# Four transposes for a tile's queries and keys, and a swapped copy written across partitions

## The chip, the cores and the metric

The kernel runs on one core of one Trainium2 chip. The metric is the device time of one execution, in microseconds (us), lower is better. The core has TensorE (PE, with its weight loads PEld), VectorE (DVE), ScalarE (ACT), GpSimd (POOL) and SyncE (SP), whose queue starts the transfers. Each takes its own instructions in order; they wait for each other by semaphores.

## The reference

A decoder of two layers on 1024 tokens of 1024 features: gated linear attention and an MLP, then differential attention and an MLP. The change is inside differential attention, eight heads, each with two components of 64 features:

```python
q = rms_norm((xn @ w_q).reshape(B, S, DIFF_HEADS, 2, DIFF_DH), q_gain) * (DIFF_DH ** -0.5)
...
s = jnp.einsum('bhcqd,bhckd->bhcqk', q_blk, k).astype(jnp.float32)
...
p = jax.nn.softmax(s, axis=-1)
a = p[:, :, 0] - lam * p[:, :, 1]
return jnp.einsum('bhqk,bhkv->bhqv', a.astype(v.dtype), v)
```

Keys are normed in the same way, and the mask is causal in blocks of 128 tokens. Float32 inputs go through the matmul as sums of a high part (rounded) and a low part (the rest).

## The kernel before

Attention runs over 64 tiles: head h, then 128 tokens t = 0 to 7. A tile is the generator `attn_tile`, cut by its `yield`s into pieces. Pieces 0 to 7 are its projection (L112 to L114: 8 groups of three matmuls); one unit of the program is the projection of one tile. The later pieces of earlier tiles are hung between the groups by the table STEPS: piece 11 of tile j stands two units later behind the second group, its scores (piece 12) a unit and a position behind that, the weighting (13), the transposes of the weights (14, L898), the product with v (15, L903) and the last scaling (16, L910) after that. PE's order is that of the program; ACT, DVE and POOL are ordered at build time by a scheduler.

The pieces that matter, in the order of their lines:

- L833 to L838: squares of q and k (ACT), sums (DVE, L836), the norm (POOL, L837, L838). L842 (DVE) multiplies, L844 (POOL) applies the gain.
- L847 to L849 write the tile `split`: for each of four blocks of 64 features (two of q, two of k) the high part, the low part, and for q once more the high part. So columns 0 to 127 of a block are [high, low], and columns 64 to 191 are [low, high].
- L854 and L857: six transposes. The two of k go to one bank of PSUM (`pk`), the four of q to another (`pq`). The pool `ms` has two banks, so a tile takes both.
- L859 (ACT) copies k to `kt`, L861 (DVE) the four columns of q to `qs`.
- L871 and L872: for each component, [high, low] of q times keys [high, low], and then [low, high] of q times the same keys. Together that is the full product.
- L881 (DVE) takes the minimum, L883 (ACT) the exponential and its sum, L888 to L891 (DVE) weigh one component against the other, L893, L907 and L908 (POOL) are the norm of the output, which L910 (ACT) applies.

At each of the seven head changes three of the next head's four weight tiles are split, and the first tile of the head after that (the first of the next head was done a head earlier): L97 loads `raw` (two buffers), L100 (POOL) multiplies it by the gains, L104 (ACT) writes the high part, L105 (DVE) the low part. The buffers of `raw` and of the weights come free only as the old head's weights are used up, so these twelve instructions and the loads fall into some 15 us. At the seventh change there is no head after the next, so there are no gains to multiply for it.

Of the kernel before, what the change touches and what calls it, by code (L numbers as in the profile page):

```python
# [6 lines left out]
F32 = mybir.dt.float32  # L7
F32R = mybir.dt.float32r
# [5 lines left out]
P = 128  # L14
# [8 lines left out]
AH, DH, VD = 8, 64, 128  # L23
# [17 lines left out]
def trunk(tc, io, out):  # L41
    nc = tc.nc
    with ExitStack() as es:
# [11 lines left out]
        def big():  # L55
            return pp.tile([P, 1024], F32, tag="big", name="big", bufs=2)
# [4 lines left out]
        def mst():  # L61
            return pp.tile([P, 512], F32, tag="ms", name="ms", bufs=2)

        def slot(name, dt=F32, shape=(P, 1024)):
            return sp.tile(list(shape), dt, tag="S", name=name, bufs=13)

        def half(name, dt=F32, shape=(P, 512)):
            return mp.tile(list(shape), dt, tag="M", name=name, bufs=16)
# [8 lines left out]
        identr = cp.tile([P, P], F32R, name="identr")  # L77
# [61 lines left out]
        def tcols(t):  # L139
            return slice(t * P, (t + 1) * P)  # L140
# [578 lines left out]
        for h in range(GH):  # L719
# [11 lines left out]
            d = 2 if h == 0 else 0  # L731
# [88 lines left out]
        def attn_tile(i):  # L820

            h, t = divmod(i, T)
            if t == 0:
                KV[h] = attn_kv()
            kt, vt = KV[h]
# [17 lines left out]
                                 s4.unsqueeze(2).broadcast_to([P, 4, DH]))  # L843
            nc.gpsimd.tensor_mul(qk[:, 0:P], qk[:, 0:P], gq)  # L844
            yield
            sp_ = slot("split", F32R)[:, 0:768].rearrange("p (a d) -> p a d", d=3 * DH)
            nc.scalar.copy(sp_[:, :, 0:DH], qk4)  # L847
            nc.vector.tensor_sub(sp_[:, :, DH:2 * DH], qk4, sp_[:, :, 0:DH].bitcast(F32))
            nc.scalar.copy(sp_[:, 0:2, 2 * DH:3 * DH], sp_[:, 0:2, 0:DH].bitcast(F32))  # L849
            yield  # L850
            pq = mst()
            pk = mst()
            for c in range(2):
                nc.tensor.transpose(pk[:, tcols(c)].bitcast(F32R), sp_[:, 2 + c, 0:P], identr)  # L854
            for c in range(2):
                for v in range(2):
                    nc.tensor.transpose(pq[:, tcols(2 * c + v)].bitcast(F32R), sp_[:, c, v * DH:v * DH + P], identr)  # L857
            for c in range(2):
                nc.scalar.copy(kt[c][:, tcols(t)], pk[:, tcols(c)])  # L859
            qs = half("qs", F32R)  # L860
            nc.vector.tensor_copy(qs, pq)  # L861
            yield
            nb = 1 if L <= 512 else 2
            B = L // nb
# [1 line left out]
            for c in range(2):  # L866
                sc = big().rearrange("p (n i) -> p n i", n=2)[:, 0:nb, 0:B]
                for n in range(nb):
                    keys = kt[c][:, n * B:(n + 1) * B]
                    lastb = n == nb - 1  # L870
                    nc.tensor.matmul(sc[:, n, :], lhsT=qs[:, tcols(2 * c)], rhs=keys, start=True, stop=False)  # L871
                    nc.tensor.matmul(sc[:, n, :], lhsT=qs[:, tcols(2 * c + 1)], rhs=keys, start=False, stop=not lastb)  # L872
                    if lastb:
                        nc.tensor.matmul(sc[:, n, B - P:B], lhsT=identb, rhs=causal, start=False, stop=True)
                scs.append(sc)
# [3 lines left out]
            for c in range(2):  # L879
                sc = scs[c]  # L880
# [9 lines left out]
            a = pr[0]  # L890
# [30 lines left out]
        def piece(j, n):  # L921
            if n == 0:
                live[j], done[j] = attn_tile(j), 0
            assert done[j] == n, (j, done[j], n)
            next(live[j])
            done[j] += 1
# [101 lines left out]
```

## Time and profile before

| | us |
|---|---|
| median of three runs | 2353.85 |
| lowest, highest | 2353.66, 2354.66 |
| the profiled execution | 2351.53 |
| its span, first to last instruction | 2349.7 |
| attention stage | about 1130 to 1640 |

The profiled execution is 2.3 us under the median. The stage is read best in periods of one head, 62.8 us each (ACT's cast L104 behind a head change starts at 1296.10, 1358.90 and 1421.70). The views used are the page, the windows, the waits and the timeline of each engine at one head change, the third (1290 to 1312 us).

### The profile page before, as it was taken

The page shows a single profiled execution, that of the slowest core. Times are in us where ns is not written, and L with a number is a line of the kernel's source. Part 1 is how long each engine was busy: PE and PEld are TensorE (multiplying, and loading weights), DVE is VectorE, ACT ScalarE, POOL GpSimd, SP SyncE. Part 2 cuts the span into 40 slices and gives each one's busy share as a digit, 9 for nine tenths or more (in the row PEclk, how much of TensorE's full clock was granted, in tenths as well). Part 3 has the DMA queues.
Part 4 walks back from the last instruction along what each step waited for, and adds up shares of the span by engine and source line. Part 5 has one row for each costly group of instructions (what it writes and reads, how often), then busy time and mean ns, then how long its engine had stood idle before and what let it go on. Part 6 is the DMA issues. An engine that isn't in the chain of part 4 may idle for free.

```text
span 2349.7 us, 31435 instructions
## 1 busy us (share of the span) xinstructions
PE 2309.7 (98%) x11710; PEld 1965.5 (84%) x11710; DVE 1490.4 (63%) x2336; ACT 1108.9 (47%) x2162; POOL 580.6 (25%) x807
## 2 busy tenths in 40 slices
PE   9999999999999999999999999999999999999999
PEld 6888888878888888887999999998878888888887
DVE  7766566478838556474666666666478838556474
ACT  6434333257335354353555555565257335354352
POOL 0253242000401103004455555543000401103002
PEclk9999999999999999999999999999999999999999
DMA  4111114667173361632101111113767173371631
GB/s 156 48 36 52 39 52 169 216 234 290 57 255 118 120 236 57 221 102 76 59 25 36 37 36 36 36 42 130 248 236 284 57 255 118 120 238 54 215 112 68
DMA packets 97831, 292.42 MB, mean 124 GB/s; under 512 B 11696, under 2 KB 24752, under 8 KB 97680
## 3 DMA queue, kind: packets, MB, share of 16 engines
q1 hardware_dynamic: 97680, 290.43, 36.1%
q8 instruction: 92, 1.51, 0.3%
q14 instruction: 59, 0.48, 0.1%
HBM read 227.47 MB, written 62.91 MB: 124 GB/s over the span
## 4 chain that ended last, share of the span: by engine, by line
PE 90%; POOL 3%; ACT 3%; DVE 2%; issue 1%; DMA 1%; SPq 0%; POOLq 0%; ACTq 0%
PE big L518 9%; PE big L522 8%; PE big L520 8%; PE mm L112 7%; PE mm L113 7%; PE mm L114 7%; PE ms L518 4%; PE ms L520 4%; PE ms L522 4%; PE mm L522 4%; PE mm L518 4%; PE mm L520 4%; PE ms L903 2%; PE big L352 2%; POOL raw L100 2%; PE big L871 1%
## 5 line engine op out<-in xcount | busy, mean ns | idle before, releaser
L518 PE MATMUL big<-oph 128*128 128x512 f32 x896 | 348.9, 389 | 0.0
L522 PE MATMUL big<-oph,opl 128*128 128x512 f32 x896 | 348.6, 389 | 0.0
L520 PE MATMUL big<-opl,oph 128*128 128x512 f32 x896 | 348.6, 389 | 0.0
L537 DVE TENSOR_TENSOR opl<-wq,oph 128x1024 fp32r<-128x1024 f32 x144 | 172.6, 1230 | 157.8 <-ACT oph L536 149.1
L537 POOL TENSOR_TENSOR opl<-hsum,oph 128x1024 fp32r<-128x1024 f32 x16 | 42.1, 2653 | 873.1 <-ACT oph L536 873.1
L536 ACT CAST oph<-wq 128x1024 fp32r<-128x1024 f32 x144 | 145.3, 1051 | 206.3 <-issue 76.8
L518 PEld LDWEIGHTS big<-oph 128*128 128x128 f32 x896 | 168.2, 188 | 35.2 <-DVE h L436 0.4
L520 PEld LDWEIGHTS big<-opl,oph 128*128 128x128 f32 x896 | 168.2, 188 | 34.9
L522 PEld LDWEIGHTS big<-oph,opl 128*128 128x128 f32 x896 | 168.2, 188 | 34.9
L112 PE MATMUL mm<-whi,x2h 128*128 128x384 f32 x512 | 188.9, 369 | 0.0
L518 PE MATMUL ms<-oph 128*128 128x512 f32 x448 | 175.2, 391 | 0.0
L520 PE MATMUL ms<-opl,oph 128*128 128x512 f32 x448 | 174.8, 390 | 0.0
L518 PE MATMUL mm<-oph 128*128 128x512 f32 x448 | 174.7, 390 | 0.0
L522 PE MATMUL ms<-oph,opl 128*128 128x512 f32 x448 | 174.6, 390 | 0.0
L522 PE MATMUL mm<-oph,opl 128*128 128x512 f32 x448 | 174.3, 389 | 0.0
L520 PE MATMUL mm<-opl,oph 128*128 128x512 f32 x448 | 174.3, 389 | 0.0
L114 PE MATMUL mm<-whi,x2l 128*128 128x384 f32 x512 | 172.4, 337 | 0.0
L113 PE MATMUL mm<-wlo,x2h 128*128 128x384 f32 x512 | 171.8, 335 | 0.0
L537 POOL TENSOR_TENSOR opl<-hc,oph 128x512 fp32r<-128x512 f32 x96 | 124.3, 1329 | 131.7 <-ACT oph L536 131.7
L536 ACT CAST oph<-ws 128x1024 fp32r<-128x1024 f32 x80 | 80.6, 1052 | 159.5 <-PE big L520 80.5
L537 DVE TENSOR_TENSOR opl<-ws,oph 128x1024 fp32r<-128x1024 f32 x80 | 94.9, 1218 | 75.8 <-ACT oph L536 75.8
L536 ACT CAST oph<-hc 128x512 fp32r<-128x512 f32 x160 | 88.2, 620 | 86.2 <-PE ms L520 58.3
(253 smaller groups left out, 5476.5 us busy)
## 6 DMA issues: line engine op xcount, KB each, us to landing
wq<-in_mlp_w SPq DMA_DIRECT2D x128, 512.0 KB, 4.6
oph<-xd SPq DMA_DIRECT2D x84, 512.0 KB, 5.9
opl<-xd SPq DMA_DIRECT2D x84, 512.0 KB, 7.2
h<-h SPq DMA_DIRECT2D x48, 512.0 KB, 4.3
xd<-oph SPq DMA_DIRECT2D x28, 512.0 KB, 3.6
xd<-opl SPq DMA_DIRECT2D x28, 512.0 KB, 4.6
raw<-in_w_qkv SPq DMA_DIRECT2D x32, 384.0 KB, 3.0
raw<-in_w_vg SPq DMA_DIRECT2D x16, 512.0 KB, 3.6
```

What stands on the lines that cost most here:

```text
L100: nc.gpsimd.tensor_mul(v, v, g)
L112: nc.tensor.matmul(ps, lhsT=l[0][ls], rhs=r[0][rs], start=first, stop=False)
L113: nc.tensor.matmul(ps, lhsT=l[0][ls], rhs=r[1][rs], start=False, stop=False)
L114: nc.tensor.matmul(ps, lhsT=l[1][ls], rhs=r[0][rs], start=False, stop=last)
L352: nc.tensor.matmul(blocks(sc, l), lhsT=w, rhs=second(w, s), start=True, stop=True)
L518: nc.tensor.matmul(banks[m], lhsT=lh[ls], rhs=rh[rs], start=one, stop=False, skip_group_check=not start)
L520: nc.tensor.matmul(banks[m], lhsT=lh[ls], rhs=rl[rs], start=False, stop=False, skip_group_check=not start)
L522: nc.tensor.matmul(banks[m], lhsT=ll[ls], rhs=rh[rs], start=False, stop=end, skip_group_check=not start)
L536: nc.scalar.copy(h_, s)
L537: eng.tensor_sub(l_, s, h_.bitcast(F32))
L871: nc.tensor.matmul(sc[:, n, :], lhsT=qs[:, tcols(2 * c)], rhs=keys, start=True, stop=False)
L903: nc.tensor.matmul(po[:, 0:P], lhsT=aT[:, tcols(j)], rhs=vt[:, j, :], start=(j == 0), stop=(j == t))
```

## The change

A tile's `split` keeps only [high, low] for each of the four blocks and moves to the pool `half`. Four transposes, keys first, write one bank (`pqk`). ACT copies the two of k. DVE copies the two of q as they are, and then partitions 64 to 127 of q to partitions 0 to 63 of the other half of `qs`; ACT copies partitions 0 to 63 to 64 to 127. That gives [low, high] without a transpose. In the built program the reads of the bank by two engines stand in a row: DVE's first copy waits for ACT's second copy of k, and ACT's copy of q waits for DVE's second.

```diff
--- before.py
+++ after.py
@@ -843,22 +843,20 @@
                                  s4.unsqueeze(2).broadcast_to([P, 4, DH]))
             nc.gpsimd.tensor_mul(qk[:, 0:P], qk[:, 0:P], gq)
             yield
-            sp_ = slot("split", F32R)[:, 0:768].rearrange("p (a d) -> p a d", d=3 * DH)
+            sp_ = half("split", F32R).rearrange("p (a d) -> p a d", d=2 * DH)
             nc.scalar.copy(sp_[:, :, 0:DH], qk4)
             nc.vector.tensor_sub(sp_[:, :, DH:2 * DH], qk4, sp_[:, :, 0:DH].bitcast(F32))
-            nc.scalar.copy(sp_[:, 0:2, 2 * DH:3 * DH], sp_[:, 0:2, 0:DH].bitcast(F32))
             yield
-            pq = mst()
-            pk = mst()
+
+            pqk = mst()
+            for a in (2, 3, 0, 1):
+                nc.tensor.transpose(pqk[:, tcols(a)].bitcast(F32R), sp_[:, a, :], identr)
             for c in range(2):
-                nc.tensor.transpose(pk[:, tcols(c)].bitcast(F32R), sp_[:, 2 + c, 0:P], identr)
-            for c in range(2):
-                for v in range(2):
-                    nc.tensor.transpose(pq[:, tcols(2 * c + v)].bitcast(F32R), sp_[:, c, v * DH:v * DH + P], identr)
-            for c in range(2):
-                nc.scalar.copy(kt[c][:, tcols(t)], pk[:, tcols(c)])
+                nc.scalar.copy(kt[c][:, tcols(t)], pqk[:, tcols(2 + c)])
             qs = half("qs", F32R)
-            nc.vector.tensor_copy(qs, pq)
+            nc.vector.tensor_copy(qs[:, 0:256], pqk[:, 0:256])
+            nc.vector.tensor_copy(qs[0:DH, 256:512], pqk[DH:P, 0:256])
+            nc.scalar.copy(qs[DH:P, 256:512], pqk[0:DH, 0:256])
             yield
             nb = 1 if L <= 512 else 2
             B = L // nb
@@ -868,8 +866,8 @@
                 for n in range(nb):
                     keys = kt[c][:, n * B:(n + 1) * B]
                     lastb = n == nb - 1
-                    nc.tensor.matmul(sc[:, n, :], lhsT=qs[:, tcols(2 * c)], rhs=keys, start=True, stop=False)
-                    nc.tensor.matmul(sc[:, n, :], lhsT=qs[:, tcols(2 * c + 1)], rhs=keys, start=False, stop=not lastb)
+                    nc.tensor.matmul(sc[:, n, :], lhsT=qs[:, tcols(c)], rhs=keys, start=True, stop=False)
+                    nc.tensor.matmul(sc[:, n, :], lhsT=qs[:, tcols(2 + c)], rhs=keys, start=False, stop=not lastb)
                     if lastb:
                         nc.tensor.matmul(sc[:, n, B - P:B], lhsT=identb, rhs=causal, start=False, stop=True)
                 scs.append(sc)

```

Behind the change lines are two lower: L879 is L881 of before, L881 is L883, L886 to L889 are L888 to L891, L891 is L893, L897 is L899, L904 to L908 are L906 to L910. L853 are the four transposes, L855 the copies of k, L857 and L858 DVE's copies of q, L859 is now ACT's copy of q.

PE's order is the same but for the transposes. The scheduler orders the other three engines anew around them. First POOL at the third head change (raw: weights before their gains; so and el: norm of the output; s: norm of q and k), before:

```order
L844 TENSOR_TENSOR qk<-qk,gq 128x128
L893 TENSOR_SCALAR el<-l 128x1
L907 TENSOR_SCALAR so<-so,el 128x1
L908 TENSOR_TENSOR so<-so,nhalf 128x1
L100 TENSOR_TENSOR raw<-raw,g_qkv 128x768
L837 TENSOR_SCALAR s_11330<-s_11330,e_b_473 128x4
L838 TENSOR_TENSOR s_11330<-s_11330,nhalf 128x4
L100 TENSOR_TENSOR raw<-raw,g_qkv 128x768
L844 TENSOR_TENSOR qk<-qk,gq 128x128
L100 TENSOR_TENSOR raw<-raw,g_qkv 128x768
L893 TENSOR_SCALAR el<-l 128x1
L907 TENSOR_SCALAR so<-so,el 128x1
```

And now:

```order
L891 TENSOR_SCALAR el<-l 128x1
L844 TENSOR_TENSOR qk<-qk,gq 128x128
L100 TENSOR_TENSOR raw<-raw,g_qkv 128x768
L905 TENSOR_SCALAR so<-so,el 128x1
L906 TENSOR_TENSOR so<-so,nhalf 128x1
L837 TENSOR_SCALAR s_11285<-s_11285,e_b_473 128x4
L838 TENSOR_TENSOR s_11285<-s_11285,nhalf 128x4
L100 TENSOR_TENSOR raw<-raw,g_qkv 128x768 x2
L891 TENSOR_SCALAR el<-l 128x1
L844 TENSOR_TENSOR qk<-qk,gq 128x128
L905 TENSOR_SCALAR so<-so,el 128x1
L906 TENSOR_TENSOR so<-so,nhalf 128x1
```

L844 went behind el, the first L100 ahead of the two instructions on so, and the second L844 and el behind both later L100.

DVE at the same place (nm: minimum of the scores; rho and p: weighing; wlo: low part of a weight), before:

```order
L861 CAST qs<-ms 128x512
L842 TENSOR_TENSOR qk<-mm,s_11210 128x256
L105 TENSOR_TENSOR wlo<-raw,whi 128x768
L881 TENSOR_REDUCE nm<-big 128x1 x2
L105 TENSOR_TENSOR wlo<-raw,whi 128x768
L888 RECIPROCAL rho<-l 128x1
L889 SCALAR_TENSOR_TENSOR rho<-rho,nlam,l 128x1
L891 SCALAR_TENSOR_TENSOR p<-p,rho 128x640
L848 TENSOR_TENSOR split<-qk,split 128x4x64
L836 TENSOR_REDUCE s_11330<-qsq 128x4
L105 TENSOR_TENSOR wlo<-raw,whi 128x768
L861 CAST qs<-ms 128x512
```

And now:

```order
L105 TENSOR_TENSOR wlo<-raw,whi 128x768
L857 CAST qs<-ms 128x256
L858 CAST qs<-ms 64x256
L879 TENSOR_REDUCE nm<-big 128x1 x2
L842 TENSOR_TENSOR qk<-mm,s_11167 128x256
L105 TENSOR_TENSOR wlo<-raw,whi 128x768
L886 RECIPROCAL rho<-l 128x1
L887 SCALAR_TENSOR_TENSOR rho<-rho,nlam,l 128x1
L889 SCALAR_TENSOR_TENSOR p<-p,rho 128x640
L848 TENSOR_TENSOR split<-qk,split 128x4x64
L105 TENSOR_TENSOR wlo<-raw,whi 128x768
L836 TENSOR_REDUCE s_11285<-qsq 128x4
```

L842 stood ahead of the first L105 and now stands behind it, the two copies of q and the two minima; the sum for s (L836) went from ahead of the third L105 to behind it.

ACT at the same place (whi: high part of a weight), before:

```order
L910 ACTIVATE oo<-ms,so 128x128
L849 CAST split<-split 128x2x64
L833 ACTIVATE qsq<-mm 128x256
L104 CAST whi<-raw 128x768
L834 ACTIVATE vt<-mm,r_b_465 128x128
L899 COPY aT<-big 128x640
L859 CAST kt<-ms 128x128 x2
L104 CAST whi<-raw 128x768
L883 ACTIVATE p,l<-big,nm 128x768 x2
L906 ACTIVATE oo,so<-ms 128x128
```

And now:

```order
L908 ACTIVATE oo<-ms,so 128x128
L104 CAST whi<-raw 128x768
L833 ACTIVATE qsq<-mm 128x256
L834 ACTIVATE vt<-mm,r_b_465 128x128
L897 COPY aT<-big 128x640
L855 CAST kt<-ms 128x128 x2
L104 CAST whi<-raw 128x768
L859 CAST qs<-ms 64x256
L881 ACTIVATE p,l<-big,nm 128x768 x2
L904 ACTIVATE oo,so<-ms 128x128
```

The third cast of a weight went ahead of the squares (qsq), and the new copy of q stands between the fourth cast and the exponentials.

## Rows read from the trace of the kernel before

**Rows 1.** Two lines of the page: the busy time of the engines (part 1), and the chain that ended last, by engine (part 4).

```profile
PE 2309.7 (98%) x11710; PEld 1965.5 (84%) x11710; DVE 1490.4 (63%) x2336; ACT 1108.9 (47%) x2162; POOL 580.6 (25%) x807
...
PE 90%; POOL 3%; ACT 3%; DVE 2%; issue 1%; DMA 1%; SPq 0%; POOLq 0%; ACTq 0%
```

**Rows 2.** The view by windows, for the stretch of the third head change and for the rest of the period behind it. Columns: stretch, its length, busy us of PE, PEld, DVE, ACT and POOL (instructions), granted clock, DMA share, GB/s.

```profile
1296.00:1312.00 16.00, 14.51 (x98) 13.53 (x97) 10.90 (x19) 10.30 (x29) 11.50 (x13) 1.00 0.33 104
1312.00:1358.00 46.00, 46.00 (x313) 43.27 (x312) 27.09 (x58) 26.68 (x89) 20.93 (x40) 1.00 0.04 11
```

**Rows 3.** The view of waits, TensorE alone, over the attention stage (1130 to 1640 us). Columns: who waited and for whom, us in total, times, longest us.

```profile
PE big L871 <- ACT aT L899: 5.3, 7, 0.8
PE ms L857 <- ACT oo L910: 2.7, 6, 0.5
PE ms L857 <- DVE x2l L469: 2.4, 2, 1.4
```

**Rows 4.** The timeline of PE (start, us, engine, line, operation, tiles, count), one tile in an undisturbed stretch: the six transposes of the split tile and the projection matmul behind them.

```profile
1319.73 0.37 PE L854 MATMUL ms<-identr,split 128*128 128x128 f32 x2
1319.94 0.50 PE L857 MATMUL ms<-identr,split 128*128 128x128 f32 x4
1320.28 0.41 PE L112 MATMUL mm<-whi,x2h 128*128 128x384 f32 x1
```

**Rows 5.** The view of groups by line and shape over the attention stage (busy us, mean ns of one, idle before and releaser): the copies that the change touches, and their nearest likes.

```profile
L861 DVE CAST qs<-ms 128x512 fp32r<-128x512 f32 x64 | 44.2, 690 | 66.9 <-PE ms L857 66.5
...
L859 ACT CAST kt<-ms 128x128 fp32r<-128x128 f32 x128 | 28.3, 278 | 8.0 <-PE ms L854 8.0
...
L842 DVE TENSOR_TENSOR qk<-mm,s 128x256 f32<-128x256 f32 x64 | 26.9, 420 | 16.8 <-POOL s L838 14.0 <-ACT p L883 2.0
...
L833 ACT ACTIVATE qsq<-mm 128x256 f32<-128x256 f32 x63 | 24.9, 395 | 0.0
```

**Rows 6.** The timeline of POOL (GpSimd) around the third head change.

```profile
1297.82 0.26 POOL L893 TENSOR_SCALAR el<-l 128x1 f32<-128x1 f32 x1 [1.89 <-ACT p L883]
...
1299.19 1.08 POOL L908 TENSOR_TENSOR so<-so,nhalf 128x1 f32<-128x1 f32 x1
...
1300.25 1.47 POOL L100 TENSOR_TENSOR raw<-raw,g_qkv 128x768 f32<-128x768 f32 x1
...
1301.82 0.27 POOL L837 TENSOR_SCALAR s<-s,e_b 128x4 f32<-128x4 f32 x1
...
1302.17 1.01 POOL L838 TENSOR_TENSOR s<-s,nhalf 128x4 f32<-128x4 f32 x1
...
1304.87 0.46 POOL L844 TENSOR_TENSOR qk<-qk,gq 128x128 f32<-128x128 f32 x1
...
1306.69 1.74 POOL L100 TENSOR_TENSOR raw<-raw,g_qkv 128x768 f32<-128x768 f32 x1 [1.36 <-ACT p L883]
...
1310.08 0.56 POOL L908 TENSOR_TENSOR so<-so,nhalf 128x1 f32<-128x1 f32 x1
```

**Rows 7.** The timeline of DVE in the same stretch.

```profile
1295.54 1.55 DVE L881 TENSOR_REDUCE nm<-big 128x1 f32<-128x640 f32 x2
...
1298.98 0.89 DVE L891 SCALAR_TENSOR_TENSOR p<-p,rho 128x640 f32<-128x640 f32 x1
...
1299.78 0.42 DVE L848 TENSOR_TENSOR split<-qk,split 128x256 fp32r<-128x256 f32 x1
...
1302.62 0.96 DVE L105 TENSOR_TENSOR wlo<-raw,whi 128x768 fp32r<-128x768 f32 x1 [1.02 <-ACT whi L104]
```

**Rows 8.** The timeline of ACT in the same stretch.

```profile
1292.98 0.86 ACT L104 CAST whi<-raw 128x768 fp32r<-128x768 f32 x1
...
1301.75 0.84 ACT L104 CAST whi<-raw 128x768 fp32r<-128x768 f32 x1 [0.60 <-POOL raw L100]
...
1304.94 0.83 ACT L104 CAST whi<-raw 128x768 fp32r<-128x768 f32 x1 [1.17 <-POOL raw L100]
```

**Rows 9.** The timeline of all engines in the same stretch: the places where PE stood still (in brackets how long, and for whom), the projection matmul that ends the stretch, and a load of raw weights on SP.

```profile
1303.49 0.44 PE L871 MATMUL big<-kt,qs 128*128 128x384 f32 x1 [0.76 <-ACT aT L899]
...
1303.61 3.85 SPq L97 DMA_DIRECT2D raw<-in_w_qkv  x2
...
1309.67 0.85 PE L898 MATMUL big<-ident,p 128*128 128x128 f32 x6 [0.29 <-DVE p L891]
...
1311.09 0.63 PE L857 MATMUL ms<-identr,split 128*128 128x128 f32 x4 [0.45 <-ACT oo L910]
...
1311.56 0.41 PE L112 MATMUL mm<-whi,x2h 128*128 128x384 f32 x1
```

**Rows 10.** The timeline of PE at its longest stop behind the attention stage.

```profile
1723.43 0.63 PE L405 MATMUL ms<-ident,ogin 128*128 128x128 f32 x4 [2.92 <-issue]
```

**Rows 11.** The view by windows right behind that stop (columns as in rows 2).

```profile
1726.00:1728.00 2.00, 2.00 (x6) 1.55 (x5) 1.05 (x2) 0.00 (x0) 0.00 (x0) 0.50 1.03 422
```

**Rows 12.** The timeline of DVE for one tile with 512 keys.

```profile
1290.34 0.75 DVE L891 SCALAR_TENSOR_TENSOR p<-p,rho 128x512 f32<-128x512 f32 x1
```

**Rows 13.** The timeline of PE for the transposes that read what the row before wrote.

```profile
1291.40 0.60 PE L898 MATMUL ms<-ident,p 128*128 128x128 f32 x4
```

**Rows 14.** The timeline of PE at the start of the stage, the two places where the transposes wait for DVE's reading of a bank.

```profile
1134.21 0.53 PE L857 MATMUL ms<-identr,split 128*128 128x128 f32 x4 [1.01 <-DVE x2l L469]
...
1141.70 0.54 PE L857 MATMUL ms<-identr,split 128*128 128x128 f32 x4 [1.36 <-DVE x2l L469]
```

## The prediction

> **What bounds the kernel now.** I read the page first, for the engine that is busy and for the chain. PE is busy for 98% of the span and makes up 90% of the chain that ended last; DVE, ACT and POOL are far from full [rows 1]. So work taken from PE should be worth its time, wherever PE doesn't wait. Then I read the windows of one head period of 62.8 us. For 46 us of it PE stands still for nothing, while DVE and ACT are each busy for 27 us and POOL for 21. In the 16 us of the head change PE is busy for 14.5 only [rows 2]. Those are two places with two limits: in the first PE alone decides, in the second a ring through POOL, ACT and DVE does. The waits of PE over the whole stage say the same: the long ones stand at the seven head changes (for the copy `aT`, 7 times, and for the scaling `oo`, 6 times), and twice at the start of the stage, where the transposes wait for a bank that DVE reads [rows 3]. Last I read the timeline of each engine through the third head change, to follow that ring.
>
> **Two transposes less, for each tile.** In an undisturbed tile the four transposes of L857 begin at 1319.94 and the next matmul at 1320.28 [rows 4]: 0.34 / 4 = 0.085 us each, 0.17 us for two. If all 64 tiles got it: 10.9 us. It is got only where PE is the last to be ready.
>
> **One tile in each head isn't.** At t = 3, DVE's weighing of 512 keys ends at 1290.34 + 0.75 = 1291.09 [rows 12], and PE's transposes that read it begin at 1291.40 [rows 13]. The slack is 0.31 us. DVE is 0.15 us busier per tile (next part), and its copies of q begin later than the one copy did, since they wait for ACT's two copies of k, so its work comes 0.2 to 0.3 us later there. I count 0.02 us for these 8 tiles, 0.2 in all.
>
> **The copies.** DVE loses a copy of 0.69 us and gains two of half the columns; ACT loses one small cast and gains one copy. The trace has no copy across partitions. From below I bound each of DVE's by half of 0.69, 0.35, and from above by its 128x256 operation on PSUM, 0.42; the new ACT copy by 0.28 (128 columns) and 0.40 (256 columns) [rows 5]. I take 0.42, since it has the same shape, and for ACT 0.30, nearer to the lower end, because the plain copy is the closer operation. That gives DVE +0.15 us per tile and ACT about nothing. New is the order at the bank: ACT's copies of k, DVE's two, ACT's one. That chain is some 1.6 us long (0.46 overlapped for k, 0.84, 0.30), and the scores that read `qs` stand a unit and a position behind, over 8 us later. The cover is the 19 us per 46 in which DVE and ACT are idle [rows 2]. So I cost the copies at nothing outside the head changes.
>
> **Waits that go.** At the start of the stage PE waits 1.01 and 1.36 us for DVE to leave a bank [rows 14]. With one bank per tile instead of two the transposes take the bank that was free. I take 2.0 of the 2.4 us, and 1.0 as the lower end, because something else may be late by then. The wait for `oo` (0.45 us at this change) goes in the same way; it is counted in the next part.
>
> **The head change, term by term.** The order of POOL, DVE and ACT differs there. I start from the cast that ends at 1292.98 + 0.86 = 1293.84 [rows 8].
> - DVE now does the low part of the weight (0.96), the two copies (0.84), the two minima (1.55) and only then L842 (0.42) [rows 5, 7]: done at 1297.6, or 1297.3 with overlaps. Before, L842 stood first.
> - POOL's next is the small norm instruction that is ready at about 1297.8 on both sides, then L844 (0.46), now behind it: until 1298.8. Then comes the multiplication by the gains, L100, that stood at 1300.25 behind L908 [rows 6]. It falls upon DVE's weighing, 0.89 us from 1298.98, and L848, which ends at 1299.78 + 0.42 = 1300.20 [rows 7].
> - Here POOL can be held up. L908 takes 0.56 us at 1310.08, but 1.08 at 1299.19, and that one ends at 1300.27, 0.07 us behind L848 [rows 6, 7]. If L100 is held in the same way it ends at 1300.2 + 1.47 = 1301.7; the two instructions on `so` follow (0.9 with gaps), ACT's scaling and then the third cast, at 1302.7. Not held up, it comes to 1301.85. Before it stood at 1301.75 [rows 8]. I take 1302.7, by the row of L908.
> - From the third cast, called S: the second scores L871 stood at 1303.49, 1.74 behind it [rows 8, 9]. The squares L833 now stand between (0.27 with overlap): S + 2.0 = 1304.7, and the 0.76 us wait for `aT` [rows 9] becomes about 2.
> - The sum for s, L836, now comes behind the third low part (S + 1.83). Then come its 0.42, L837 and L838 (0.27 and 1.01), L100 (1.47) [rows 6]: the fourth cast at S + 5.1. From the fourth cast to the next transposes of weights, L898, it was 1309.67 - 1304.94 = 4.73 us [rows 8, 9]; the new copy of q adds 0.30, L844 (0.46) waits for an L100 whose load takes 3.08 us (1303.61 to 1306.69) [rows 6, 9], which fits in that. So L898 at S + 10.0: 1311.9 to 1312.7 instead of 1309.67, 2.2 to 3.0 us late.
> - From L898 to the projection L112 it was 1311.56 - 1309.67 = 1.89 us; without the wait for `oo` and two transposes 0.96. That gives back 0.93.
> - Net +1.3 to +2.1 us for each change; I take 1.9, as the third cast is held by the nearest row. Six changes: +11.4. The seventh has no such L100 behind it; there only the third cast's delay counts, +0.85 (0.3 to 1.2).
>
> The step about L908 meets a page of the Trainium skill. "SBUF — State Buffer", section "Terms", says that DVE and GpSimd share a pair of ports, taken for a whole instruction, and that the loser is blocked altogether. The rows agree for L908. By that rule, taken alone, the third cast is at 1302.7 and the sum is the one below; without it the cast is at 1301.85 and the sum about 6 us lower (7 x 0.85).
>
> **The sum.** Inside the seven comparisons stand 21 tiles, three each, and 8 are the short ones: 64 - 21 - 8 = 35 tiles with 0.17 us, -5.95; -0.2; start of the stage -2.0; six changes +11.4; the seventh +0.85. Together +4.1 us. The profiled execution of before took 2351.53 us, 2.3 us under the median: 2355.6 there, and 2358.0 against the median of 2353.85. With the ends of the terms: 6 x 1.3 + 0.3 - 6.0 - 0.2 - 2.4 = -0.5, and 6 x 2.1 + 1.2 - 6.0 - 0.2 - 1.0 = +6.6. So this case by itself lies at 2353 to 2361.
>
> **Rival 1, faster: the new order at the head changes costs nothing.** For it: PE is 98% busy, the chain is PE for 90%, and POOL, DVE and ACT have room [rows 1, 2]. Then the two transposes of 64 tiles (-10.9), the starts (-2.4) and the waits for `oo` (-2.7) [rows 3] give -16, or -10 if the short tiles and half of the waits stay: 2338 to 2344. Against it: in the 16 us of the head change POOL is busy for 11.5 [rows 2], PE waits there already for what POOL feeds, and L844 and L100 changed places. It decides where the third cast stands: at 1301.75 or earlier.
>
> **Rival 2, slower: the longer stops take the clock down.** Behind the attention stage, PE stood still for 2.92 us [rows 10], and right behind it the granted clock fell to 0.50, the lower of its two levels, 1.2 instead of 2.4 GHz [rows 11]. The head change with its stops of 0.76 and 0.45 us shows 1.00 [rows 2, 9]. The new stops of about 2 us before L871 and L898 lie between. The row is 2 us at half speed, so 1 us lost; with a part of the stretch on either side of it I take 1.7; at six changes +10, 2368. It decides if one of the windows behind a head change shows a clock below 1.00.
>
> **Rival 3, slower: the chain at the bank is not covered.** If DVE's copies, waiting for ACT's copies of k, hold up the minimum and the weighing behind them, the tiles with few keys are hit: t = 3 and t = 2 have the least time from scores to weights. Two tiles in each of eight heads by 0.3 us: +4.8, 2363. For it speaks the slack of 0.31 [rows 12, 13]; against it the 46 us without a wait of PE [rows 2]. It decides if PE waits for `p` at L898 outside the head changes.
>
> **How the numbers follow.** The measurement can tell about 0.2%, 4.7 us, from no change: 2349.1 to 2358.6 is the same. The forecast has 0.58; by its own range about 0.03 of it falls under the bound, 0.31 within, and 0.24 above, as its middle lies close to the upper edge. Rival 1 has 0.26, all faster; rivals 2 and 3 0.08 each, slower. Together faster 0.29, same 0.31, slower 0.40. The range is 2340 to 2364: it takes in the forecast, rival 3 and most of rival 1, and leaves out rival 2 and the lower end of rival 1, about 0.15.
>
> **What would show it.** In the changed profile: L853 with four transposes per tile and 0.17 us less before the next matmul; a head period in which the 46 us are about 0.7 us shorter (0.17 for four to five tiles) and the head change 1 to 2 us longer; PE waiting about 2 us each for `aT` and for `p` at six changes, and no longer for `oo` or for `x2l`; the third cast of a head change behind both L908 and L100; the copies at 0.35 to 0.42 us. It is wrong if PE's waits at the head changes are not longer than before, if DVE's copies across partitions take well over 0.42 us, or if the granted clock falls in the stage.

## The result and the profile after

| | us |
|---|---|
| median after (5 runs) | 2378.11 |
| lowest, highest | 2373.53, 2379.00 |
| median before, the same chips (5 runs) | 2353.85 |
| ratio after to before, 95% interval | 1.010, 1.0087 to 1.0114 |
| the profiled execution of after, its span | 2378.83, 2377.0 |

The change made the kernel 24.3 us slower. The forecast was 2358.0, in a range of 2340 to 2364.

The page of after, its busy times and its chain by engine, against [rows 1]:

```profile
PE 2307.5 (97%) x11582; PEld 1954.8 (82%) x11582; DVE 1514.2 (64%) x2400; ACT 1120.3 (47%) x2162; POOL 578.4 (24%) x807
...
PE 82%; DVE 5%; ACT 5%; POOL 4%; issue 2%; DMA 1%; SPq 0%; ACTq 0%; POOLq 0%; DVEq 0%
```

PE is busy for 2.2 us less, and still the span is 27.3 us longer: what was added is waiting. PE's share of the chain fell from 90 to 82%, and DVE's, ACT's and POOL's rose. The waits of PE over the attention stage (1130 to 1665 us now; L896 are the transposes of the weights, L898 before, and L869 the scores, L871 before) say for whom:

```profile
PE big L896 <- DVE p L889: 26.4, 14, 3.3
PE big L869 <- ACT aT L897: 7.2, 14, 0.8
PE ms L896 <- DVE p L889: 3.5, 16, 0.2
```

In [rows 3] the longest sums were 5.3, 2.7 and 2.4 us. The waits for `oo` and `x2l` are gone, as forecast. In their place stand 26.4 us for DVE's weighing `p`, two at each head change, and 3.5 us in 16 short waits for the same thing.

Since PE's order is the same, the start of each tile's first transpose of weights can be set side by side. This table is worked out from the timelines of PE: us from that start in the tile before to the one in this tile, for the third head period and, last, its sum. The columns e1 to e12 are experiments of the next section.

```
tile         before  after   e1     e5     e7     e10    e11    e12
t=1           5.79    5.63   5.61   5.63   5.66   6.26   5.67   5.67
t=2           4.23    4.61   4.61   4.61   4.23   4.23   4.26   4.27
t=3           6.90    7.16   7.15   7.15   6.73   6.76   6.74   6.72
t=4           8.72    9.89   8.51   8.90   8.84   8.43   8.45   8.38
t=5           9.55   11.53  11.24  10.26   9.95  10.01   9.10   9.09
t=6           9.38    8.47   8.47   8.64   9.10   8.47   8.47   8.41
t=7           9.18    9.18   9.18   9.22   9.01   9.01   9.02   9.01
t=0, next     9.05    9.20   9.19   9.18   8.95   8.96   8.93   8.86
period       62.80   65.67  63.96  63.59  62.47  62.13  60.64  60.42
```

The head change lies in t = 4 and 5 (and what it gives back in t = 6). There the stops are. The same change in the timelines of after, PE first, then DVE, POOL and ACT:

```profile
1301.67 0.63 PE L896 MATMUL ms<-ident,p 128*128 128x128 f32 x4 [0.23 <-DVE p L889]
...
1311.56 0.74 PE L896 MATMUL big<-ident,p 128*128 128x128 f32 x5 [1.32 <-DVE p L889]
...
1314.75 0.44 PE L869 MATMUL big<-kt,qs 128*128 128x384 f32 x1 [0.79 <-ACT aT L897]
...
1323.09 0.84 PE L896 MATMUL big<-ident,p 128*128 128x128 f32 x6 [2.45 <-DVE p L889]
...
1324.07 0.41 PE L112 MATMUL mm<-whi,x2h 128*128 128x384 f32 x1
...
1309.36 2.06 DVE L889 SCALAR_TENSOR_TENSOR p<-p,rho 128x640 f32<-128x640 f32 x1
...
1309.27 1.47 POOL L100 TENSOR_TENSOR raw<-raw,g_qkv 128x768 f32<-128x768 f32 x1
...
1310.72 1.08 POOL L905 TENSOR_SCALAR so<-so,el 128x1 f32<-128x1 f32 x1
...
1312.74 0.82 ACT L104 CAST whi<-raw 128x768 fp32r<-128x768 f32 x1
...
1317.88 0.83 ACT L104 CAST whi<-raw 128x768 fp32r<-128x768 f32 x1 [2.85 <-POOL raw L100]
```

From the transposes of t = 3 (1301.67) to L112 behind the change (1324.07) it takes 22.40 us; before it was 1311.56 - 1291.40 = 20.16 [rows 9, 13]. The first stop, 1.32 us, comes from a pair of rows: L100 on POOL began at 1309.27, and DVE's weighing L889 0.09 us later. It lasted 2.06 us instead of 0.89 [rows 7] and ended 0.68 us behind L100. The second stop, 2.45 us, stands at the end of the ring: the third cast at 1312.74, the fourth at 1317.88 (5.14 us behind it), L896 another 5.21 us on.

Outside the head change there is the tile t = 2. After, the four transposes of a later tile, whose copies stand ahead of the minimum of t = 2 on DVE; ACT's copies of k, DVE's two of q, the minimum, the scaling of rho (L887) beside POOL's L844, and the wait of PE at the end:

```profile
1289.01 0.46 PE L853 MATMUL ms<-identr,split 128*128 128x128 f32 x4
...
1289.50 0.43 ACT L855 CAST kt<-ms 128x128 fp32r<-128x128 f32 x2 [0.98 <-PE ms L853]
...
1289.97 0.43 DVE L857 CAST qs<-ms 128x256 fp32r<-128x256 f32 x1 [1.90 <-ACT kt L855]
...
1290.41 0.43 DVE L858 CAST qs<-ms 64x256 fp32r<-64x256 f32 x1
...
1291.19 1.02 DVE L879 TENSOR_REDUCE nm<-big 128x1 f32<-128x384 f32 x2
...
1293.24 0.46 POOL L844 TENSOR_TENSOR qk<-qk,gq 128x128 f32<-128x128 f32 x1 [0.24 <-DVE rho L886]
...
1293.25 0.46 DVE L887 SCALAR_TENSOR_TENSOR rho<-rho,nlam,l 128x1 f32<-128x1 f32 x1
...
1294.51 0.52 PE L896 MATMUL ms<-ident,p 128*128 128x128 f32 x3 [0.23 <-DVE p L889]
```

And the kernel before, the six transposes' second group, DVE's copy of q and the minimum at the same place:

```profile
1279.31 0.52 PE L857 MATMUL ms<-identr,split 128*128 128x128 f32 x4
...
1279.87 0.69 DVE L861 CAST qs<-ms 128x512 fp32r<-128x512 f32 x1 [1.21 <-PE ms L857]
...
1281.12 1.03 DVE L881 TENSOR_REDUCE nm<-big 128x1 f32<-128x384 f32 x2 [0.23 <-PE big L874]
```

Before, DVE began 0.04 us behind the last transpose (1279.31 + 0.52). Now it begins 0.50 us behind (1289.01 + 0.46), when ACT has copied k, and takes 0.85 us for two copies instead of 0.69; its minimum begins 1.72 us behind the end of the transposes instead of 1.29, and PE waits 0.23 us for the weighing that hangs on it (by the table t = 2 is 0.38 us longer). Another 0.24 us of the way comes from L887, which took 0.46 us beside POOL's L844 where its median is 0.22; e7 below has that too (0.45), and no such wait. At t = 3 L887 takes 0.22 us, and PE waits 0.23 as well. The groups by line and shape over the stage give the copies' durations, and the weighing at t = 4:

```profile
L857 DVE CAST qs<-ms 128x256 fp32r<-128x256 f32 x64 | 27.2, 424 | 80.3 <-ACT kt L855 79.3
...
L858 DVE CAST qs<-ms 64x256 fp32r<-64x256 f32 x64 | 27.2, 426 | 0.9
...
L859 ACT CAST qs<-ms 64x256 fp32r<-64x256 f32 x64 | 23.4, 365 | 31.9 <-DVE qs L858 30.7
...
L889 DVE SCALAR_TENSOR_TENSOR p<-p,rho 128x640 f32<-128x640 f32 x8 | 15.3, 1910 | 0.2
```

A copy across 64 partitions costs what one of 128 partitions costs on DVE (426 and 424 ns). But the copy L857 has 79 us of idle time ahead of it that ends with ACT's copies of k.

Last, the granted clock, the view by windows behind the second stop of the fourth and of the fifth change (granted clock third from the end):

```profile
1390.00:1392.00 2.00, 2.00 (x8) 1.50 (x8) 1.17 (x3) 1.61 (x6) 0.48 (x1) 0.55 0.00 0
1392.00:1394.00 2.00, 2.00 (x9) 1.52 (x9) 1.17 (x3) 0.64 (x2) 1.28 (x2) 0.60 0.00 0
...
1455.00:1457.00 2.00, 1.02 (x11) 1.05 (x11) 0.83 (x1) 0.51 (x2) 1.38 (x2) 1.00 0.18 59
1457.00:1459.00 2.00, 2.00 (x13) 1.73 (x12) 0.96 (x3) 1.61 (x6) 0.41 (x1) 1.00 0.00 0
```

Both follow a stop of 2.46 us, at 1386.3 and 1453.5. Behind one the granted clock fell to 0.55 and 0.60 in two windows, towards the lower of its two levels (0.50, 1.2 instead of 2.4 GHz [rows 11]); behind the other it stayed at 1.00. It fell at three of the seven changes; t = 6 then takes some 10.0 us instead of 8.47, about 1.55 us more.

### The profile page after: what moved, and what is told of

It reads as the page before. It is cut to its first block, busy times and chain, and to the rows that moved or that the text cites. A ratio compares the mean times of both kernels' runs of the same rounds, so it can differ in the third digit from the quotient of the medians.

```text
span 2377.0 us, 31316 instructions
## 1 busy us (share of the span) xinstructions
PE 2307.5 (97%) x11582; PEld 1954.8 (82%) x11582; DVE 1514.2 (64%) x2400; ACT 1120.3 (47%) x2162; POOL 578.4 (24%) x807
## 4 chain that ended last, share of the span: by engine, by line
PE 82%; DVE 5%; ACT 5%; POOL 4%; issue 2%; DMA 1%; SPq 0%; ACTq 0%; POOLq 0%; DVEq 0%
PE big L518 8%; PE big L520 8%; PE big L522 8%; PE mm L112 6%; PE mm L113 6%; PE mm L114 6%; PE ms L518 4%; PE ms L520 4%; PE ms L522 4%; PE mm L522 4%; PE mm L518 4%; PE mm L520 4%; PE big L352 2%; ACT p L881 2%; PE ms L901 1%
## 5 line engine op out<-in xcount | busy, mean ns | idle before, releaser
L112 PE MATMUL mm<-whi,x2h 128*128 128x384 f32 x512 | 189.0, 369 | 0.0
```

Of the source, the lines that this page charges most:

```text
L112: nc.tensor.matmul(ps, lhsT=l[0][ls], rhs=r[0][rs], start=first, stop=False)
```

## The experiments

Theory A: POOL's order at the head change is the loss. Theory B: the order of the copies in the one bank is, ACT's of k first. Theory C: the copies across partitions are. The ratios are to the kernel before, beside which each ran.

**e1 and e2: POOL's order alone.** POOL's instructions of the stage are tied in a row, in an order given by letters: s, S are L837 and L838, G is L844, W is L100, e, o and O are L893, L907 and L908. At a head change before has `sSGeoOWsSWGWeoOWs`, after has `sSeGWoOsSWWeGoOWs`. e1 is after with the order of before, e2 the kernel before with the order of after.

```diff
-                nc.gpsimd.tensor_mul(v, v, g)
+                rec("W", nc.gpsimd.tensor_mul(v, v, g))
...
+        for k in POOL_ORDER:
+            ins = RECS[k][seen.setdefault(k, 0)]
+            seen[k] += 1
+            if prev is not None:
+                tc.add_manual_dep(ins, prev.name, mybir.DependencyInfo(
+                    mybir.DependencyClass.NoSync, mybir.DependencyReason.DATA), reason="pool order")
+            prev = ins
```

> The changed kernel, with POOL's instructions of the attention stage put into the order of the kernel before (L844 ahead of el, the third L100 behind the two on so, L844 between the later L100); copies and transposes as changed. Theory A (POOL's order at the head change is the loss: L100 runs into DVE's weighing, PE waits 1.3 and 2.5 us at L896, and the clock falls behind the longer stops): both waits go, some 2.7 us for each of seven changes and the falls of the clock, so 2353 to 2360. Theory B (the copies of k ahead of those of q in one bank make DVE late in every tile): POOL's order matters little, 2370 or more, and the 0.23 us waits at t = 2 and t = 3 stay in any case.

Measured: 2358.99 us, 1.0026 (1.0015 to 1.0036), 19 us less than after. The head period is 63.96 and no window behind a change shows a fallen clock. So theory A has the larger part of the loss: 1.7 us of each period, and the falls of the clock, which go with the stops. But 1.16 us per period against before stay, and the waits at t = 2 and t = 3 stay as they were (table). The edit ties POOL alone, but the scheduler, which still orders DVE and ACT, then also put the sum for s (L836) back ahead of the third low part and the squares back ahead of the third cast; the 1.7 us hold these two steps as well.

> The kernel before, six transposes and its own copies, with POOL's instructions in the order of the changed kernel. Theory A: PE waits for p at both L898 of a head change as in the changed kernel, slower by about 7 x 2.5 us and a fall of the clock or two, 2368 to 2376. Theory B: within 5 us of the kernel before.

Measured: 2362.83 us, 1.0052 (1.0035 to 1.0069), +9.4 us where theory A said 15 to 22. The order by itself costs, but half of what it costs with the new copies. Only the first stop came, 0.84 to 1.01 us at six of the seven changes; the second is 0.2 us, and the clock fell behind none. DVE kept its order of before here.

**e3 and e4: four transposes with one plain copy.**

```diff
-            nc.vector.tensor_copy(qs[:, 0:256], pqk[:, 0:256])
-            nc.vector.tensor_copy(qs[0:DH, 256:512], pqk[DH:P, 0:256])
-            nc.scalar.copy(qs[DH:P, 256:512], pqk[0:DH, 0:256])
+            nc.vector.tensor_copy(qs.rearrange("p (r c) -> p r c", r=2), pqk[:, 0:256].unsqueeze(1).broadcast_to([P, 2, 256]))
```

In e4 this line stands ahead of ACT's copies of k.

> The changed kernel with one DVE copy that writes the unswapped columns twice, in place of the three copies across and along partitions; ACT's copy of q is gone. It leaves the exchange of high and low out of q's second form. The order at the head change is that of the changed kernel, and the copies of k still come ahead. Theory A and theory B both: the loss stays, 2365 to 2376. Theory C (the copies across partitions, and ACT's wait for DVE, are the loss): 2350 or less.

Measured: 2358.19 us, 1.0022 (1.0012 to 1.0032). All three theories missed; the loss is neither kept nor gone. The weighing at t = 4 is 1911 ns long here too, so POOL's order still does its harm, yet the period is 63.65, 2.0 us under that of after. That bounds the price of DVE's second copy and ACT's third in a row with the others. It isn't measured alone: the scheduler also put ACT's third cast ahead of the output's scaling here, where after has it behind.

> As the run with the plain copy, but DVE's copy of q is written ahead of ACT's copies of k, so that it starts with the last transpose, as in the kernel before; it leaves out the same exchange. POOL's order at the head change is then nearly that of the kernel before. Theories A and B: four transposes give their 0.17 us in nearly all tiles and the waits are those of before, 2340 to 2347. Theory C says the same here. If it stays above 2352, something else in the four transposes costs.

Measured: 2356.48 us, 1.0017 (1.0007 to 1.0026). It stayed above 2352, with POOL's order at the head change that of before and no copy across partitions: PE waits for `p` 21 times, 17.1 us in all. These waits stand at t = 5, 6 and 7 (0.88, 0.94 and 0.77 us), not at t = 2 and t = 3, which take 4.23 and 6.73 us. The scheduler ordered DVE anew here: it put L842, which waits for POOL's norm, ahead of the minimum (L877 here), in t = 6 for instance:

```profile
1316.50 0.42 DVE L842 TENSOR_TENSOR qk<-mm,s 128x256 f32<-128x256 f32 x1 [1.50 <-POOL s L838]
1316.84 2.08 DVE L877 TENSOR_REDUCE nm<-big 128x1 f32<-128x896 f32 x2
```

So e4 tells of an order of DVE, and doesn't show by itself that one bank costs; that is left to runs with the orders held.

**e5, e6, e7: all three orders of before, and the bank.** DVE's and ACT's instructions are tied in the same way. e5 is after with the orders of before (L849 is gone, DVE's second copy stands behind its first, ACT's copy of q ahead of the exponentials). In e6 DVE's copies are written ahead of ACT's. In e7 k and q have a bank each:

```diff
+            pk = mst()
             pqk = mst()
-            for a in (2, 3, 0, 1):
-                nc.tensor.transpose(pqk[:, tcols(a)].bitcast(F32R), sp_[:, a, :], identr)
             for c in range(2):
-                nc.scalar.copy(kt[c][:, tcols(t)], pqk[:, tcols(2 + c)])
+                nc.tensor.transpose(pk[:, tcols(c)].bitcast(F32R), sp_[:, 2 + c, :], identr)
+            for c in range(2):
+                nc.tensor.transpose(pqk[:, tcols(c)].bitcast(F32R), sp_[:, c, :], identr)
             qs = half("qs", F32R)
+            for c in range(2):
+                nc.scalar.copy(kt[c][:, tcols(t)], pk[:, tcols(c)])
```

> The changed kernel with POOL, DVE and ACT all put into the order of the kernel before (ACT's copy of q stands ahead of the exponentials); copies of k still ahead of those of q. If the order of all three engines is the loss, apart from the 0.23 us waits at t = 2 and t = 3 that come from the order of the copies in the bank: a clean head period of some 62.3 us against 62.8 of before, 2346 to 2354. If the copies themselves are the loss, the period stays near the 63.97 of the run with POOL's order alone, 2357 to 2361.

Measured: 2358.28 us, 1.0021 (1.0012 to 1.0030): no faster than e1 beyond the intervals, though the period is 0.37 us shorter in the profiles.

> As the run with all three orders of before, but DVE's two copies of q ahead of ACT's two of k. If the copies of k are what makes DVE late at t = 2 and t = 3, those waits (0.23 us each) go and the head period falls by 0.6 to 0.9 us against that run: 2341 to 2348. If not, the two runs give the same.

Measured: 2364.99 us, 1.0048 (1.0035 to 1.0060), slower than e5 where a gain was expected. t = 2 and t = 3 take 5.08 and 7.62 us: now ACT's copies of k wait for DVE's, with the exponentials behind them on ACT. The view of waits, ACT alone (L893 are the copies of k, L891 DVE's second copy):

```profile
ACT kt L893 <- DVE qs L891: 50.6, 50, 1.8
```

Theory B was wrong in that it blamed who goes first; it is the row itself, as e7 shows.

> As the run with all three orders of before, but k and q each in a bank of its own again, so that DVE doesn't wait for ACT; each tile takes both banks, and the waits for oo (0.45 us a change) and for x2l (2.4 us in all) are back. Then as with q first plus some 5 us: 2344 to 2352.

Measured: 2351.20 us, 0.9985 (0.9976 to 0.9994). With e5 it differs by the bank alone: 1.12 us of each period, of which t = 2 and t = 3 have 0.8.

**e8 and e9: the stop at t = 4.** e8 is after, in its own order, with L100 in three instructions. e9 is after with one step of POOL's order undone, `GWoO` to `GoOW`.

```diff
-                nc.gpsimd.tensor_mul(v, v, g)
+                for a in range(3):
+                    rec("W", nc.gpsimd.tensor_mul(v[:, :, a], v[:, :, a], g[:, :, a]))
```

> The changed kernel in its own order on POOL, but L100 in three instructions of 256 columns each. If DVE's weighing lasts 2.06 us because it waits for the whole of an L100 of 1.47 us, it now waits for a third of it at most: 1.2 to 1.5 us long, the 1.33 us wait of PE at the first transposes of weights falls under 0.7, and the time by 4 to 10 us, to 2368 to 2374. If the weighing is late for another reason, nothing changes or, as three instructions take longer, it gets slower.

Measured: 2383.56 us, 1.0131 (1.0115 to 1.0146), 5.5 us slower than after where a gain of 4 to 10 was expected. The groups by line and shape of e8:

```profile
L902 DVE SCALAR_TENSOR_TENSOR p<-p,rho 128x640 f32<-128x640 f32 x8 | 9.3, 1163 | 0.2
...
L113 POOL TENSOR_TENSOR raw<-raw,g_qkv 128x256 f32<-128x256 f32 x75 | 53.4, 743 | 2.9 <-DMA raw<-in_w_qkv 1.7 <-DVE p L902 1.2
```

The weighing did what was expected, 1163 ns against 1910, PE's first wait fell to 0.47 us, and t = 4 took 9.03 us instead of 9.89. But three pieces of 743 ns take 2.2 us where one took 1.5, and the second stop grew: t = 5 12.96 us instead of 11.53.

> The changed kernel with one step of POOL's order undone at each head change: the first L100 behind the two instructions on so instead of ahead of them; the rest of POOL's order is the changed one (the scheduler then also puts the sum for s ahead of the third low part again). If it is that L100 into which DVE's weighing runs, the weighing for the tile with 640 keys is back to some 0.9 us and PE's wait of 1.33 us at its transposes goes (8.5 us from the transposes of t = 3 instead of 9.9), the clock no longer falls at each second change, and the time is 2358 to 2366. If the delay of L844 and the later L100 is the larger part, the second wait (2.46 us) stays and the time is 2366 to 2374.

Measured: 2368.72 us, 1.0075 (1.0055 to 1.0095); its runs lie between 2364.94 and 2376.90. The weighing is 884 ns and t = 4 takes 8.72 us; the first stop is gone. The second stayed (t = 5: 11.65), and the clock still fell behind it, in the profiled run (the slowest of the four, 2376.90) at four changes. The time lies in the range of the second theory, but the later L100 and L844 are not the larger part of the loss. The third period, without a fall of the clock, takes 65.67 us in after, 64.58 here and 63.96 in e1: 1.09 us for the first L100 (with the two steps of DVE and ACT that the scheduler took back here as in e1), 0.62 for the rest of POOL's order. In the medians each step is about half of the 19 us, since the falls of the clock stayed with the second stop.

**e10, e11, e12: two banks.** e10 is after with a bank each (the diff of e7) and nothing tied. e11 is e7 with ACT's copy of q ahead of the weight's cast, and the L100 that stood ahead of the output's norm (`sSWGWeoOWs`) behind it (`sSWGeoOWWs`). e12 is e11 with both copies across partitions on ACT:

```diff
-            nc.vector.tensor_copy(qs[0:DH, 256:512], pqk[DH:P, 0:256])
+            nc.scalar.copy(qs[0:DH, 256:512], pqk[DH:P, 0:256])
```

> The changed kernel with k and q each in a bank of its own, and nothing else: the order of DVE, ACT and POOL is the scheduler's. No wait of DVE's copies for ACT's, so the 0.23 us waits at t = 2 and t = 3 go; the scheduler puts POOL's third L100 behind so by itself here, but two L100 side by side behind the output's norm. If the bank alone is most of the loss, 2350 to 2356; if the pinned orders are needed as well, 2356 to 2364.

Measured: 2345.56 us, 0.9971 (0.9961 to 0.9981), 32.5 us less than after, more than all three orders brought, and under both ranges. The edit is the second bank alone, but the scheduler ordered all three engines anew around it, so this is not the price of the bank; that is e5 to e7, 1.12 us of a period. The third period is 62.13 us, the three behind it 61.7.

> The run with two banks and the orders of before, with two steps more: ACT's copy of q ahead of the cast of a weight (it was behind, ahead of the exponentials), and POOL's L100 that falls upon DVE's weighing of the 768 keys behind the output's norm instead of ahead of it. Each takes some 0.25 to 0.35 us from the chain to the transposes of t = 4 and t = 5: a period of 61.9 to 62.2 instead of 62.46, 2347 to 2350.

Measured: 2338.73 us, 0.9944 (0.9932 to 0.9956), more than was expected: the period fell by 1.83 us, not by 0.3 to 0.6.

> As the tuned run with two banks, but ACT makes both copies across partitions and DVE only the one along them: DVE loses 0.42 us per tile against that run (0.27 against the kernel before), ACT gains 0.36. If the tiles with few keys are limited by DVE's chain, t = 2 gets its 0.17 us too and the period is 61.5 to 62.0, 2344 to 2348. If ACT, which is on the same chain with its exponentials, becomes the limit, it is slower than the tuned run.

Measured: 2337.26 us, 0.9934 (0.9922 to 0.9946). It is under the range that was expected; it beats both kernels, and e11 by no more than the intervals allow. The waits of PE over the stage (to 1640 us), first e10, then e12:

```profile
PE big L899 <- DVE p L892: 10.7, 8, 2.1
PE ms L856 <- ACT oo L911: 3.2, 7, 0.5
PE ms L856 <- DVE x2l L469: 1.9, 2, 1.2
```

```profile
PE big L907 <- ACT aT L935: 7.0, 7, 1.0
PE ms L501 <- DVE x2l L504: 1.9, 1, 1.9
```

In e12 the waits for `p` and `oo` at the head changes are gone as well; the one for `aT`, 1.0 us each, is left. t = 2 did not get its 0.17 us, and couldn't: between the transposes of weights of t = 1 and those of t = 2 PE's program has no transposes of q and k, in no kernel here (in the kernel before, none from 1280.27 to 1284.50).

## Why the prediction was wrong

**The transposes: right.** In the table t = 1 falls by 0.16 us, and PE's stretch around each tile's four transposes by 0.16 to 0.18. **The waits that go: right.** `oo` and `x2l` are gone, and the start of the stage, to its first transposes of weights, came 3.7 us sooner relative to what lies ahead of it, where I had 2.0.

**The head change: near in sum, in part by luck.** Reckoned from the transposes of t = 3, the third cast was forecast 11.3 us on and stood at 11.07, the second scores 13.3 and 13.08, the second transposes of weights 20.5 to 21.3 and 21.42, L112 21.4 to 22.3 and 22.40. The net is +2.24 us for a change, and I had taken +1.9 out of 1.3 to 2.1. What I had not seen is the first stop. From the row of L908 I made POOL the one that is held up by DVE. In after L100 was there 0.09 us before DVE, and it was DVE that was held, with PE behind it; e9 and e8 show this. The third cast stood near its forecast by luck: L100 wasn't held and ended 9.07 us on, not 10.3, but then L905 met the weighing and took 1.08 us instead of its usual 0.27. The wait for `aT` behind it, forecast at about 2 us, stayed at 0.79, since the first stop stands ahead of it. "SBUF — State Buffer" of the Trainium skill, section "SBUF: two separate sides", says that whoever starts first has the ports for the whole instruction; the rows agree in both directions, 1.08 us for L908 and 2.06 for L889.

**The step that failed: "So I cost the copies at nothing outside the head changes".** I took the idle share of DVE and ACT, 19 us of 46, as cover. An average doesn't cover a chain: PE waits for what hangs on the copies at t = 2 and t = 3 (0.23 us each), and for `aT` at t = 0 (0.24 us). Of a period, 65.67 - 62.80 = 2.87 us is lost; 2.24 of it is the head change, so the rest of the period lost 0.63 us where I had it gain 0.87. Over seven periods that is 10.5 us, the largest part of the miss. (t = 2 has no transposes of q and k to lose; at t = 7 the 0.17 us saved are waited away again: 9.18 us in before and after, 9.01 in e7.) It is the mechanism of rival 3; its price, 4.8 us, was half of it, and it was kept apart from the forecast with 0.08. e7 against e5 shows its cause: the row of copies in one bank, 1.12 us of a period. "PSUM — Partial Sum Buffer" of the Trainium skill, section "PSUM bank collisions raise a hardware error", says that no two engines may read one bank in the same partitions at the same time, while different groups of 32 partitions may be read side by side. By that rule ACT's copies of k and DVE's first copy have to wait for each other, but DVE's second copy and ACT's copy of q, which read different halves of the partitions, would not; in after ACT's copy still waits for DVE's second (30.7 us over the stage). No run here tried them side by side.

**The rivals were no alternatives.** Rival 2, the clock, came as well: three falls of about 1.55 us, 4.7 us, where I had 1.7 for each of six. All three slower cases held together, and a sum over them with the terms above would have been near 2373 (2358 + 10 + 4.8).

**The seventh change** has no L100 behind its third cast, and still its period grew by 3.09 us (64.67 against 61.58), not by 0. I had counted the third cast alone; the first L100 meets the weighing there too (t = 4 takes 9.89 us), and a second stop of 1.50 us is left. The first change lost 0.8 us more than the others (its second stop is 3.28 us long); why wasn't tried.

The sum by periods: 6 x 2.87 + 3.09 + 4.65 (clock) + 0.8 (first change) = 25.8 us. The profiled span grew by 27.3. The same matmuls of both profiles, set side by side, give the rest: -3.7 at the start of the stage, +1.4 in the last head and behind it, and +3.9 ahead of the stage, nearly all before 510 us, where the change alters no line. There PE has a wait that no other profile here shows, with the clock at 0.54 and 0.61 in the two windows behind it:

```profile
505.83 0.56 PE L518 MATMUL big<-oph 128*128 128x512 f32 x1 [2.52 <-DVE h L436]
```

So these 3.9 us belong to this execution, not to the change; the medians differ by 24.3. What brought that wait stays open.

What is shown of the causes, in us of a head period: POOL's order 1.7 (after to e1, with the two steps that follow it), the rest of DVE's and ACT's order 0.37 (e1 to e5, in the profiles only), the shared bank 1.12 (e5 to e7). Together that is the way from after to e7, 3.20 us, which ends 0.33 under the period of before. With the scheduler free, the second bank brings 3.5 to 4 us (after to e10), and how much of that is the bank's own isn't separated.

## What to carry to other kernels

A buffer that is saved by putting the results of two readers into one bank sets the readers in a row; before that is costed at nothing, follow the one consumer that waits behind the row, in the shortest tile, not the mean idle time of the engine. When an edit lets a scheduler order the engines anew, compare its order at the tightest place with the old one, and tie the old order down: tying POOL alone gave back 19 us of 24 here, while a second bank, with the scheduler free to order anew around it, gave 32.5. Cases that can hold at the same time belong into one sum.

## What was not expected of the hardware

Where an instruction of DVE with two inputs and L100 on POOL met in these rows, the one that began second ended behind the other, whatever its own length: in after L889, which began 0.09 us later. In e1 it happened at another place, and there the second began 0.55 us later. The timelines of POOL and DVE (L112 there is L100, L899 the scaling of rho, L889 before):

```profile
1308.48 1.47 POOL L112 TENSOR_TENSOR raw<-raw,g_qkv 128x768 f32<-128x768 f32 x1
...
1309.03 0.94 DVE L899 SCALAR_TENSOR_TENSOR rho<-rho,nlam,l 128x1 f32<-128x1 f32 x1
```

L899 has one column, and its median in the kernel before is 0.22 us; here it ended 0.02 us behind L112's end. DVE's copies between partition halves cost no more than plain ones (426 ns), ACT's 365 ns. And of the five stops of 2.45 to 2.46 us in after, two are followed by a lower clock and three are not.
